# One hybrid transformer step: four mixers and their projections move from the framework's scheduler into the kernel's own list schedule

## The chip, the cores and the metric

The kernel runs on one core of a Trainium2 chip. The core has five engines, each with its own in-order stream: TensorE (PE, matmuls, with PEld for the loading of weights), VectorE (DVE), ScalarE (ACT), GpSimd (POOL) and SyncE (SP), which here issues nearly all transfers. The metric is the device time of one execution in microseconds (us).

## The reference

The reference computes one layer of a diffusion backbone on 128 context tokens and 512 latent tokens (640 rows of 1024 values):

```
h    = rmsnorm(x) * (1 + scale1) + shift1          # shift, scale, gate: silu(c) @ ada_w
proj = h @ w_in                                     # 1024 x 3360, split among four mixers
A: HGRN2 gated linear recurrence, both directions   (q, i, f_fwd, f_bwd, g)
B: GLA gated linear attention, both directions      (q, k, v, g, a_fwd, a_bwd)
C: RG-LRU recurrence after a 4-tap convolution      (x, gate)
D: short convolution, b * conv(c * v)
x = x + gate1 * (concat(A, B, C, D) @ w_out)
x = x + gate2 * (relu(rmsnorm(x)-modulated @ w1)^2 @ w2)
y = rmsnorm(x)
```

It returns y for all rows and the final states of A, B and C. Every matmul works on fp32 data; the large ones split each operand into a rounded part and a remainder and add three products (hi x hi, hi x lo, lo x hi).

## The kernel before, in words

**Three stages.** In the first one, up to about 58 us, the rows are normalised, transposed and modulated into `hhi` and `hlo` (the two parts of h, with channels on the partitions), and two of the thirteen projections (`a0`, `q`) are computed in a PE order that is written out by hand (`START`). The second stage, from 58 to 325 us, holds the other projections and the four mixers. The third holds the output projection, the second norm and the MLP.

**The second stage.** Each projection chunk is 256 columns of `w_in`. `need` loads it (SP, tile `raw...`), `prep` makes `hi...` and `lo...` of it on ACT or DVE, and `proj_cm` multiplies it with `hhi` and `hlo`: 48 matmuls of 320 columns for 128 outputs, into one of two PSUM buffers of the tag `mm` (tiles `pj...`; `v...` for values). A `use_...` function then reads that buffer out: `use_db`, for example, is three DVE multiplications from PSUM (L848 to L850). The mixers A (two jobs) and B (one job of two head pairs) run a recurrence as a tree of eight levels, 1 to 128: at each level copies build `K` and `Qb` from the array `G` (on ACT or DVE, by the table `ON_DVE`), PE computes scores `sA` or `sB` with small matmuls, DVE merges them under a mask (`copy_predicated` into `W`) and multiplies `G` by the decays (L944, L945). After level 128 come the state updates (`kt`, `ds`, `St`), the readout `o` and a norm over heads (`hn`). C has small block matmuls (`rg`), activations and scans. `ada` units compute the modulation vectors with matmuls (`ap`).

**Two kinds of matmul on PE.** A projection uses all 128 columns of the array. The scores, the `ap` matmuls, `pjba` and parts of `ds` and `o` write 32 or 64 partitions only, and two or four of these run side by side on different columns.

**What sets the order.** The list `PLAN` says in which order the units are written: a projection unit such as `cx0`, or one step of a job (`A0`, `A1`, `RG`, `B`). In the kernel before, the units of `PLAN` are handed straight to the framework, whose scheduler orders the instructions of each engine. The third stage is different: its operations are recorded in a `Plan`, a list scheduler inside the kernel. `cost` gives each operation a duration by formulas, `record` keeps it with its operands, `add` finds which earlier operations touch the same elements, and `emit` computes for each operation the latest time at which it must begin, walks through time, and at each moment gives the engine that is free first the ready operation with the least such time. `Late` tiles stand for tiles that are allocated only when they are emitted. `Slots` are the buffers of a tag, in the order in which their users were recorded. What `emit` puts out is kept in that order (`manual_schedule`). In the third stage the order on PE is fixed by the program (`plan.chain`).

**The weights of the output projection.** `wo_v` and `wo_x` load `w_out` through two buffers `w2raw` and four buffers `wq`, on the same SP queue as the projections' weights.

Of the kernel before, what the change touches and what calls it, by code (L numbers as in the profile page):

```python
# [13 lines left out]
D = 1024  # L14
# [131 lines left out]
class Plan:  # L146

    def __init__(self, nc, like):  # L150
        self.nc, self.like, self.ops, self.seen, self.masks = nc, like, [], {}, {}
        self.chain, self.last_pe, self.hint, self.tiles_of = False, None, None, {}
# [80 lines left out]
    def record(self, eng, fn, op, a, k):  # L233
# [12 lines left out]
        def go():  # L246
            r = lambda x: x.real() if isinstance(x, Late) else x
            return fn(*[r(x) for x in a], **{w: r(v) for w, v in k.items()})  # L248

        return self.add(eng, dur, go, ins, outs, mb, sets)  # L250

    def add(self, eng, dur, fn, ins=(), outs=(), mb=0.0, sets=None, after=()):
# [16 lines left out]
        for k in keys:  # L269
            if isinstance(k, LateTile):  # L270
                if not k.users:
                    k.slots.queue.append(k)
                    if k.pool.opened is not None:
                        order.add(k.pool.opened)
                k.users.append(i)
                k.pool.users.append(i)
# [16 lines left out]
    def emit(self):  # L293
# [115 lines left out]
def hybrid_step_kernel(ctx: ExitStack, tc: tile.TileContext, A: dict, O: dict):  # L409
# [42 lines left out]
    def lnexp(after):  # L452
        with tc.issue_after(after.ins):
            ld = act.preload_act_table_set("natural_log_exp_and_others")
        with tc.issue_after(ld.ins):
            yield

# [251 lines left out]
    me_, ml_ = ExitStack(), ExitStack()  # L709
    me = me_.enter_context(tc.tile_pool(name="mixe", bufs=1, reuse_waits="tile"))  # L710
    mp = ml_.enter_context(tc.tile_pool(name="mixl", bufs=1, side="right", reuse_waits="tile"))

# [5 lines left out]

    def sub(t, g, off, ap):
        v = t[:, g, off:off + 1]  # L720
        return bass.AP(tensor=v.tensor, offset=v.offset, ap=[list(v.ap[0])] + ap)
# [488 lines left out]
    for u in PLAN:  # L1210
# [10 lines left out]
        if u == "q1":  # L1221
            psS_stack.close()
            psB = stB.enter_context(tc.tile_pool(name="psB", bufs=2, space=PS, reuse_waits="tile"))
    grow1 = gate_rows("gt1", nc.sync)
    for j in jobs.values():
        assert next(j, None) is None
    me_.close()
    lp = ctx.enter_context(tc.tile_pool(name="mlp", bufs=1, reuse_waits="tile"))
    oT["hi"] = [lp.tile([128, 2, T], F32R, name=f"ohi{i}", tag=f"ohi{i}") for i in range(4)]
    oT["lo"] = [lp.tile([128, T], F32R, name=f"olo{i}", tag=f"olo{i}") for i in range(8)]  # L1230
    for j in range(2):
        put_o(4 + j, [(slice(0, 128), hs[j][:, 0:128]), (slice(128, T), hs[j][:, 134:646])])
# [4 lines left out]
    for j in range(2):  # L1237
        put_o(6 + j, [(ALL, dd["o", j])])
    ml_.close()
    hw_.close()  # L1240
    plan = Plan(nc, par[:, 0:1].tensor)
    rp = LatePool(plan, ctx.enter_context(tc.tile_pool(name="mlpr", bufs=1, side="right", reuse_waits="tile")))
    ls = LatePool(plan, ctx.enter_context(tc.tile_pool(name="mlps", bufs=1, reuse_waits="tile")))
    stB.close()
    psA_.close()
    psN = LatePool(plan, ctx.enter_context(tc.tile_pool(name="psN", bufs=1, space=PS, reuse_waits="tile")), psum=True)
    lp = LatePool(plan, lp)
    VH, VL = ([lp.tile([128, D], F32R, name=f"{nm}{i}", tag=f"{nm}{i}") for i in range(4)] for nm in ("vh", "vl"))
    BIG = [lp.tile([128, D], F32, name=f"big{i}", tag=f"big{i}") for i in range(2)]
    WRAW2 = [lp.tile([128, D], F32, name=f"w2raw{i}", tag=f"w2raw{i}") for i in range(2)]  # L1250
    act, dve, pe, pool, sync = (Now(e) for e in (act, dve, pe, pool, nc.sync))

# [32 lines left out]
    def wo_x(i, k0):  # L1285
        for k in range(2):
            s = [k0 + 2 * k, k0 + 2 * k + 1]
            wo[2 * i + k] = [(XH[j], XL[j]) for j in s]
            for n, j in enumerate(s):
                raw = WQ[2 * k + n]  # L1290
                sync.dma_start(raw, A["wout"][i][:, D * k + 512 * n:D * k + 512 * n + 512])
                split(XH[j], XL[j], raw)

    def wo_v(i, k0):
        for k in range(2):
            j = k0 + k
            sync.dma_start(WRAW2[k], A["wout"][i][:, D * k:D * k + D])
            split(VH[j], VL[j], WRAW2[k])
# [5 lines left out]
    wo_x(3, 4)  # L1304
    act, dve, pe, pool = plan.engines()
    nc = Queues(plan, nc)
    last_used = [2, 0, 3, 1]
# [455 lines left out]
```

## Time and profile before

| what | value |
|---|---|
| median of 3 runs | 824.52 us (822.47 to 827.32) |
| profiled execution: its own time | 819.71 us |
| profiled execution: span | 817.9 us |
| PE busy | 778.8 us, 95% |
| DVE busy | 575.2 us, 70% |
| ACT busy | 420.3 us, 51% |
| granted clock of PE, mean | 0.997 |

The times of the table are of whole executions; the trace is of one of them, and its span runs from its first instruction to its last, 1.8 us less than its own time. A busy share is the union of an engine's instructions. The rows of the trace name an engine, a line (L249 or L248 is the line of the recording layer, through which many operations go), an operation, and the tile written and the tiles read, without buffer numbers.

### The profile page before, as it was taken

The numbers are of one execution on the slowest core, as the hardware profiler recorded it, in microseconds if no ns is written. First come the engines' busy times: TensorE is split into PE (matmuls) and PEld (weight loads), VectorE is DVE, ScalarE is ACT, GpSimd is POOL, SyncE is SP. The second block draws the span as 40 slices with busy tenths as digits, with TensorE's granted clock in tenths as the row PEclk, the third lists the DMA queues.
The fourth block names the chain that finished last, engine by engine and source line by source line (L and its number), as shares of the span: only waits on it lengthen the run. The fifth ranks groups of instructions, "written<-read, shape, count | busy, mean of one in ns | idle before, by whom it ended". The sixth has DMA issues, their size and how long they took to land.

```text
span 817.9 us, 13749 instructions
## 1 busy us (share of the span) xinstructions
PE 778.8 (95%) x5536; PEld 682.7 (83%) x5536; DVE 575.2 (70%) x1061; ACT 420.3 (51%) x708; POOL 23.4 (3%) x48
## 2 busy tenths in 40 slices
PE   4999999999999989999899999899999999999995
PEld 3798988768777889888888989789899898998984
DVE  4779988857786376368997888647466475675757
ACT  7533549688486332156784706417246172371533
POOL 0040000101010000000000000000000000000001
PEclk9999999999999999999999999999999999999998
DMA  9723323333321522543653636513132041330313
GB/s 352 304 83 137 105 95 142 116 110 100 125 84 56 104 103 65 194 155 127 204 165 102 195 97 204 119 40 117 50 131 75 20 136 52 101 106 2 128 52 128
DMA packets 33696, 97.79 MB, mean 120 GB/s; under 512 B 8672, under 2 KB 9696, under 8 KB 29024
## 3 DMA queue, kind: packets, MB, share of 16 engines
q1 hardware_dynamic: 32544, 95.72, 35.5%
q10 hardware_dynamic: 576, 1.00, 0.4%
q8 instruction: 43, 0.70, 0.3%
q0 software_dynamic: 512, 0.20, 0.1%
q14 instruction: 21, 0.17, 0.1%
HBM read 91.44 MB, written 5.46 MB: 118 GB/s over the span
## 4 chain that ended last, share of the span: by engine, by line
PE 63%; DVE 15%; ACT 10%; DMA 8%; issue 3%; SPq 0%; DVEq 0%; ACTq 0%
PE ps L248 45%; DMA wq<-in_w_dram 4%; ACT QbB L462 2%; DVE xl L248 2%; PE pjcx L492 2%; PE pjdb L492 2%; PE pja L666 2%; DMA w2raw<-in_wout_dram 1%; PE ap L536 1%; DVE wq L248 1%; DMA w2raw<-in_w_dram 1%; PE pjbqk L492 1%; DVE big L248 1%; PE rg L1132 1%; DMA rawdb<-in_win_dram 1%
## 5 line engine op out<-in xcount | busy, mean ns | idle before, releaser
L248 PE MATMUL ps<-vh,olo 128*128 128x512 f32 x680 | 186.4, 390 | 1.0 <-DVE olo L248 0.7
L248 PEld LDWEIGHTS ps<-vh,olo 128*128 128x128 f32 x680 | 126.9, 188 | 28.8 <-DVE olo L248 1.9
L248 PE MATMUL ps<-vl,olo 128*128 128x512 f32 x320 | 99.3, 390 | 0.0
L248 ACT ACTIVATE vh<-w2raw 128x1024 fp32r<-128x1024 f32 x32 | 33.8, 1057 | 118.6 <-PE ps L248 114.2
L248 ACT ACTIVATE xh<-wq 128x512 fp32r<-128x512 f32 x96 | 59.4, 628 | 61.1 <-PE ps L248 43.9
L248 PE MATMUL ps<-yh,xh 128*128 128x320 f32 x256 | 79.5, 311 | 1.2 <-DVE rb L248 1.2
L248 PE MATMUL ps<-yl,xh 128*128 128x320 f32 x256 | 79.0, 309 | 0.0
L248 PE MATMUL ps<-yh,xl 128*128 128x320 f32 x256 | 79.0, 308 | 0.0
L248 DVE TENSOR_TENSOR h<-ps,h 128x512 f32<-128x512 f32 x60 | 38.6, 686 | 52.9 <-PE ps L248 52.6
L248 PEld LDWEIGHTS ps<-vl,olo 128*128 128x128 f32 x320 | 60.1, 188 | 12.7
L248 DVE TENSOR_TENSOR xl<-wq,xh 128x512 fp32r<-128x512 f32 x96 | 64.8, 687 | 8.1 <-ACT xh L248 7.9
L248 PE MATMUL ps<-ohi,xh 128*128 128x320 f32 x256 | 57.1, 310 | 0.5 <-ACT xh L248 0.4
L248 ACT ACTIVATE rb<-rb 128x640 f32<-128x640 f32 x64 | 46.8, 734 | 7.6 <-DVE rb L248 6.8
L248 PEld LDWEIGHTS ps<-yh,xh 128*128 128x128 f32 x256 | 48.1, 188 | 2.0 <-DVE rb L248 1.5
L248 PEld LDWEIGHTS ps<-yl,xh 128*128 128x128 f32 x256 | 48.1, 188 | 0.3
L248 PEld LDWEIGHTS ps<-yh,xl 128*128 128x128 f32 x256 | 48.1, 188 | 0.0
L248 DVE TENSOR_TENSOR vl<-w2raw,vh 128x1024 fp32r<-128x1024 f32 x32 | 39.0, 1220 | 8.1 <-ACT vh L248 7.4
L248 PEld LDWEIGHTS ps<-ohi,xh 128*128 128x128 f32 x256 | 42.8, 188 | 1.1 <-ACT xh L248 0.6
L248 PE MATMUL ps<-ohi,xl 128*128 128x320 f32 x128 | 39.8, 311 | 0.5 <-DVE xl L248 0.4
L248 DVE TENSOR_TENSOR olo<-rb,olo 128x640 fp32r<-128x640 f32 x32 | 26.3, 821 | 18.6 <-ACT olo L248 18.6
L248 PE MATMUL ps<-t,xh 128*128 128x320 f32 x128 | 28.7, 311 | 0.7 <-DVE rb L248 0.7
L248 ACT ACTIVATE rb<-ps 128x320 f32<-128x320 f32 x64 | 27.1, 424 | 4.1 <-PE ps L248 4.1
(426 smaller groups left out, 1677.7 us busy)
## 6 DMA issues: line engine op xcount, KB each, us to landing
ar<-in_ada_w_dram SPq DMA_DIRECT2D x20, 1024.0 KB, 4.9
wq<-in_w_dram SPq DMA_DIRECT2D x72, 256.0 KB, 3.7
w2raw<-in_w_dram SPq DMA_DIRECT2D x32, 512.0 KB, 4.4
big<-in_ada_g_dram SPq DMA_DIRECT2D x8, 512.0 KB, 3.5
x<-in_x_dram SPq DMA_DIRECT2D x5, 512.0 KB, 6.8
big<-in_x_dram SPq DMA_DIRECT2D x5, 512.0 KB, 4.2
x1d<-big SPq DMA_DIRECT2D x5, 512.0 KB, 2.6
xa<-x1d SPq DMA_DIRECT2D x5, 512.0 KB, 4.5
```

What stands on the lines that cost most here:

```text
L248: return fn(*[r(x) for x in a], **{w: r(v) for w, v in k.items()})
L462: act.activation(out, src, AF.Copy)
L492: pe.matmul(ps[:, n, :320], wt[:, k, c0:c0 + 128], h[:, k, s], start=(k == 0 and wt is hi and h is hhi), stop=stop)
L536: pe.matmul(ps[32 * g:32 * g + 32, :256], scx[:, 4 * j + g, 2 - 2 * vi:34 - 2 * vi], r3[:, 4 * j + g, :], start=(vi == 0 and j == 0), stop ...
L666: pe.matmul(d, w[:, k, 128 * j:128 * j + 128], (hlo if hi_ else hhi)[:, k, c], start=begin, stop=end, skip_group_check=(ch == "q" and i == 1))
L1132: pe.matmul(ps, wrg[:, dl, j, g, :], xc[:, hN * n:hN * n + hN], start=True, stop=True)
```

## The change

The `Plan` is made before the mixers, and everything from the second stage on is recorded in it: the projections with their loads and splits, the mixers, the `ada` units, the output projection and the MLP. The two pools of the mixers, the weight pool and the PSUM pools become `LatePool`s. Pools that are closed and opened between the stages become events in the plan: `open_lp` after the last operation that uses the pool `me`, `open_rest` and `open_psum` after the last ones of the others.

- The projections that the first stage leaves unread get release times (`ready`: "pja0" at 7.5, "pjq" at 18.4 us on the plan's own clock), and the engines get the times at which they come free (`free`).
- The first operation that uses a tile must now stand before its others, and when several tiles share one buffer, a tile is due no later than the next one's first use.
- The table loads for logarithms on ACT are no longer placed by hand; `lnexp` sets a hint.
- `ON_DVE` is the same, so each copy stays on its engine. The PE order is free in the second stage and fixed in the third, as it was. No operation is added or left out, but for ACT's table loads, of which 27 stand in the program where 29 stood.

```
-    def __init__(self, nc, like):
+    def __init__(self, nc, like, ready=(), free=None):
+        self.ready, self.free, self.first = dict(ready), dict(free or {}), {}
...
+        for x in ins:
+            if not isinstance(x, Late):
+                for name, t in self.ready.items():
+                    if x.tensor.name.startswith(name):
+                        self.first[len(self.ops)] = t
...
+                elif k.users[0] != i:
+                    order.add(k.users[0])
...
+        before = {}
+        for x in slots:
+            for p, q in zip(x.queue, x.queue[1:]):
+                before.setdefault(q.users[0], []).append(p.users[0])
         for i in range(n - 1, -1, -1):
             eng, dur, _, deps, order, mb, _ = ops[i]
+            for d in before.get(i, ()):
+                if d < i:
+                    latest[d] = min(latest[d], latest[i])
...
-        at, free, ready, end_of = [0.0] * n, {}, {}, [0.0] * n
+        at, free, ready, end_of = [self.first.get(i, 0.0) for i in range(n)], dict(self.free), {}, [0.0] * n
...
+    plan = Plan(nc, par[:, 0:1].tensor, ready={"pja0": 7.5, "pjq": 18.4}, free={"PE": 18.2, "ACT": 7.5, "DVE": 8.4})
+    me = LatePool(plan, me_.enter_context(tc.tile_pool(name="mixe", bufs=1, reuse_waits="tile")))
+    mp = LatePool(plan, ml_.enter_context(tc.tile_pool(name="mixl", bufs=1, side="right", reuse_waits="tile")))
+    real_nc, const0 = nc, const
+    act, dve, pe, pool = plan.engines()
+    nc = Queues(plan, nc)
+    const, wpool, psA = LatePool(plan, const0), LatePool(plan, wpool, bufs=2), LatePool(plan, psA, psum=True, bufs=2)
...
+    def open_psum():
+        stB.close()
+        psA_.close()
+        psN.real = ctx.enter_context(tc.tile_pool(name="psN", bufs=1, space=PS, reuse_waits="tile"))
+
+    rp.opened = ls.opened = plan.event(open_rest, [lp.opened] + wpool.users + mp.users + on_rows)
+    psN.psum = True
+    psN.opened = plan.event(open_psum, psA.users + psB.users + on_first)
```

How the order moves is shown at three places.

**The readout of mixer B's second head pair, on PE.** `oB` is the readout; its `64x128` matmuls write one half of the partitions each, and two of them make a pair. `pjdc`, `pjdb` and `pjdv` are projections of mixer D. Before:

```order
L1053 MATMUL oB_3041<-TB_2118,vbv 64x128 x2
L1047 MATMUL oB_3041<-GB,StB_2771 128x128
L1049 MATMUL oB_3041<-GB,StB_2771 128x128
L1053 MATMUL oB_3041<-TB_2118,vbv 64x128 x2
L492 MATMUL pjdc_3061<-hlo,hidc 128x320
```

Now the readout stands near the end of the stage, among two projections that alternate:

```order
L249 MATMUL pjdb_3381<-hhi,hidb 128x320
L249 MATMUL oB_3299<-TB_2724,vbv 64x128
L249 MATMUL pjdb_3381<-hhi,hidb 128x320
L249 MATMUL oB_3299<-TB_2724,vbv 64x128
L249 MATMUL pjdv_3342<-hlo,hidv 128x320
L249 MATMUL oB_3299<-GB,StB_2315 128x128
L249 MATMUL pjdb_3381<-hlo,hidb 128x320
L249 MATMUL pjdv_3342<-hlo,hidv 128x320
```

A pair that stood together is parted by a projection's matmul, and two projections are computed in turns where before one ended ahead of the other.

**The SP queue at the end of the stage.** `rawdv` and `rawdb` are the last two weight chunks of the projections, `w2raw` and `wq` the weights of the output projection, `rowgt` a row of gates, `big` rows of x. Before:

```order
L472 DMA rawdv<-in_win_dram 128x2048
L561 DMA rowgt_3476<-gt_76 128x8x1 x2
L130 DMA w2raw_3529<-in_wout_dram 128x1024
L130 DMA w2raw_3535<-in_wout_dram 128x1024
L130 DMA w2raw_3529<-in_wout_dram 128x1024
L130 DMA w2raw_3535<-in_wout_dram 128x1024
L472 DMA rawdb<-in_win_dram 128x2048
```

Now:

```order
L249 DMA rawdv<-in_win_dram 128x2048
L249 DMA rawdb<-in_win_dram 128x2048
L249 DMA rowgt_611<-gt_76 128x8x1 x2
L249 DMA w2raw_3419<-in_wout_dram 128x1024
L249 DMA w2raw_3423<-in_wout_dram 128x1024
L249 DMA big_3425<-in_x_dram 128x1024
```

`rawdb` no longer stands behind four loads of `w_out`.

**The join of the second and the third stage, on PE.** `hnb` is the head norm of mixer B, `pjdb` the last projection, and `ps` the output projection. Before, `hnb` stands 78 projection matmuls ahead of this piece's last row:

```order
L492 MATMUL pjdb_3423<-hhi,hidb 128x320 x2
L492 MATMUL pjdb_3423<-hlo,hidb 128x320 x2
L492 MATMUL pjdb_3423<-hhi,lodb 128x320 x2
L248 MATMUL ps_0_3605<-vh_3531,ohi_3485 128x512
L248 MATMUL ps_1_3613<-vh_3531,ohi_3485 128x512
```

Now:

```order
L249 MATMUL pjdv_3342<-hhi,lodv 128x320
L249 MATMUL pjdb_3381<-hhi,lodb 128x320
L249 MATMUL pjdb_3381<-hhi,hidb 128x320 x2
L249 MATMUL pjdb_3381<-hlo,hidb 128x320 x2
L249 MATMUL pjdb_3381<-hhi,lodb 128x320 x2
L249 MATMUL pjdb_3381<-hhi,hidb 128x320 x2
L249 MATMUL pjdb_3381<-hlo,hidb 128x320 x2
L249 MATMUL hnb_3519<-o2b_3451,con 128x320
L249 MATMUL hnb_3524<-o2b_3451,con 128x320
L249 MATMUL pjdb_3381<-hhi,lodb 128x320 x2
L249 MATMUL pjdb_3381<-hhi,hidb 128x320 x2
L249 MATMUL pjdb_3381<-hlo,hidb 128x320 x2
```

After two more matmuls of `pjdb` the row `ps_0` follows. The projection `pjdv`, which ended 48 matmuls before `ps`, ends 19 matmuls and the two of `hnb` before it. From that row to the end PE's order is the same in both kernels.

## Rows read from the trace of the kernel before

**Rows 1.** Busy time by stage: PE, PEld, DVE, ACT, POOL, granted clock, DMA share, GB/s.
```profile
0.00:58.20 58.20, 45.42 (x368) 38.62 (x369) 36.75 (x87) 32.38 (x56) 10.00 (x25) 1.00 0.64 254
58.20:325.00 266.80, 254.81 (x2587) 218.30 (x2586) 201.09 (x388) 154.98 (x248) 10.95 (x22) 1.00 0.31 101
60.00:160.00 100.00, 97.92 (x1248) 86.35 (x1248) 92.19 (x189) 58.15 (x96) 4.08 (x6) 1.00 0.36 125
325.00:420.00 95.00, 91.65 (x489) 79.53 (x489) 70.80 (x128) 52.28 (x103) 0.00 (x0) 1.00 0.51 174
420.00:817.90 397.90, 386.95 (x2098) 346.21 (x2097) 266.59 (x460) 180.62 (x302) 2.41 (x1) 0.99 0.32 99
```

**Rows 2.** Waits of PE, 58.2 to 325 us: total, times, longest (us).
```profile
PE sB L962 <- ACT QbB L462: 3.1, 7, 0.7
PE pjdb L492 <- DVE lodb L483: 1.4, 1, 1.4
...
PE sB L989 <- issue: 0.9, 2, 0.7
PE pjdb L492 <- DVE hidb L460: 0.9, 1, 0.9
PE sA L962 <- DVE QbA L460: 0.8, 2, 0.5
...
PE sB L962 <- DVE QbB L460: 0.5, 2, 0.3
PE sA L989 <- ACT QbA L462: 0.5, 1, 0.5
PE pjdv L492 <- DVE sgb L813: 0.5, 1, 0.5
```

**Rows 3.** SP's issues, 40 to 340 us: start, length of the group, queue, transfer.
```profile
274.02 14.41 SPq L130 DMA_DIRECT2D w2raw<-in_wout_dram  x4
290.96 0.33 SPq L472 DMA_DIRECT2D rawdb<-in_win_dram  x1
```

**Rows 4.** Timeline of PE, first and last of a `pjdb` stretch: start, length, instruction.
```profile
317.93 0.46 PE L492 MATMUL pjdb<-hhi,hidb 128*128 128x320 f32 x2
...
324.68 0.46 PE L492 MATMUL pjdb<-hhi,lodb 128*128 128x320 f32 x2
324.97 0.63 PE L248 MATMUL ps<-vh,ohi 128*128 128x512 f32 x2
```

**Rows 5.** Timeline of PE, one score block among projections.
```profile
64.96 0.46 PE L492 MATMUL pja<-hhi,loa 128*128 128x320 f32 x2
65.35 0.77 PE L962 MATMUL sA<-QbA,KA 128*32 128x64 f32 x40
66.05 0.56 PE L492 MATMUL pja<-hhi,hia 128*128 128x320 f32 x2
66.44 0.45 PE L492 MATMUL pja<-hlo,hia 128*128 128x320 f32 x2
```

**Rows 6.** Timeline of PE, two score blocks that follow each other.
```profile
92.05 0.28 PE L863 MATMUL vi<-loi,hhi 128*128 128x256 f32 x1
92.17 0.28 PE L864 MATMUL vi<-hii,hlo 128*128 128x256 f32 x1
92.38 1.32 PE L962 MATMUL sA<-QbA,KA 128*32 128x64 f32 x80
93.63 0.56 PE L492 MATMUL pjcx<-hhi,hicx 128*128 128x320 f32 x2
94.03 0.46 PE L492 MATMUL pjcx<-hlo,hicx 128*128 128x320 f32 x2
```

**Rows 7.** Timeline of PE, a level of mixer B and what it waits for.
```profile
205.74 0.85 PE L962 MATMUL sB<-QbB,KB 128*32 128x128 f32 x20 [0.61 <-ACT QbB L462]
```

**Rows 8.** Timeline of DVE, the readout of the last two projections of mixer D.
```profile
318.13 0.29 DVE L832 TENSOR_TENSOR du<-dc,pjdv 128x128 f32<-128x128 f32 x1 [0.26 <-PE pjdv L492]
...
319.79 1.84 DVE L840 SCALAR_TENSOR_TENSOR dy<-du,par,dy 128x656 f32<-128x656 f32 x2
325.17 0.29 DVE L848 TENSOR_TENSOR od<-dy,pjdb 128x128 f32<-128x128 f32 x1 [3.55 <-PE pjdb L492]
...
325.64 0.48 DVE L850 TENSOR_TENSOR od<-dy,pjdb 128x320 f32<-128x320 f32 x1
```

**Rows 9.** Timeline of PE and of DVE: mixer B's head norm.
```profile
309.63 1.24 PE L1071 MATMUL hnb<-o2b,con 128*128 128x320 f32 x4
312.89 0.82 DVE L1077 TENSOR_TENSOR orB<-orB,o2b 128x640 f32<-128x640 f32 x1
```

More of the change, by code (lines that the diff above doesn't have):

```diff
@@ L452, in lnexp @@
     def lnexp(after):
[L453 to L456, printed above, removed]
+        plan.hint = "natural_log_exp_and_others"
+        yield
+        plan.hint = None
     def cp(name, out, src):
@@ L709, in hybrid_step_kernel @@
     me_, ml_ = ExitStack(), ExitStack()
-    me = me_.enter_context(tc.tile_pool(name="mixe", bufs=1, reuse_waits="tile"))
-    mp = ml_.enter_context(tc.tile_pool(name="mixl", bufs=1, side="right", reuse_waits="tile"))
+    plan = Plan(nc, par[:, 0:1].tensor, ready={"pja0": 7.5, "pjq": 18.4}, free={"PE": 18.2, "ACT": 7.5, "DVE": 8.4})
[5 more added lines that the diff above has]
+    const, wpool, psA = LatePool(plan, const0), LatePool(plan, wpool, bufs=2), LatePool(plan, psA, psum=True, bufs=2)
     def tmp(nm):
@@ L719, in sub @@
     def sub(t, g, off, ap):
+        if isinstance(t, Late):
+            return t.view(lambda x: sub(x, g, off, ap))
         v = t[:, g, off:off + 1]
@@ L1221, in hybrid_step_kernel, with open_psB, open_lp @@
         if u == "q1":
-            psS_stack.close()
-            psB = stB.enter_context(tc.tile_pool(name="psB", bufs=2, space=PS, reuse_waits="tile"))
+            def open_psB():
+                psS_stack.close()
+                psB.real = stB.enter_context(tc.tile_pool(name="psB", bufs=2, space=PS, reuse_waits="tile"))
+            psB = LatePool(plan, psum=True, bufs=2)
+            psB.opened = plan.event(open_psB, range(len(plan.ops)))
     grow1 = gate_rows("gt1", nc.sync)
+    on_rows = on_first = list(range(len(plan.ops)))
     for j in jobs.values():
         assert next(j, None) is None
-    me_.close()
-    lp = ctx.enter_context(tc.tile_pool(name="mlp", bufs=1, reuse_waits="tile"))
+    lp, rp, ls, psN = (LatePool(plan) for _ in range(4))
+    def open_lp():
+        me_.close()
+        lp.real = ctx.enter_context(tc.tile_pool(name="mlp", bufs=1, reuse_waits="tile"))
+    lp.opened = plan.event(open_lp, me.users)
     oT["hi"] = [lp.tile([128, 2, T], F32R, name=f"ohi{i}", tag=f"ohi{i}") for i in range(4)]
     oT["lo"] = [lp.tile([128, T], F32R, name=f"olo{i}", tag=f"olo{i}") for i in range(8)]
+    VH, VL = ([lp.tile([128, D], F32R, name=f"{nm}{i}", tag=f"{nm}{i}") for i in range(4)] for nm in ("vh", "vl"))
+    BIG = [lp.tile([128, D], F32, name=f"big{i}", tag=f"big{i}") for i in range(2)]
+    WRAW2 = [lp.tile([128, D], F32, name=f"w2raw{i}", tag=f"w2raw{i}") for i in range(2)]
     for j in range(2):
@@ L1238, in hybrid_step_kernel, with open_rest @@
         put_o(6 + j, [(ALL, dd["o", j])])
[L1239 to L1251, printed above, removed]
+    def open_rest():
+        ml_.close()
+        hw_.close()
+        rp.real = ctx.enter_context(tc.tile_pool(name="mlpr", bufs=1, side="right", reuse_waits="tile"))
+        ls.real = ctx.enter_context(tc.tile_pool(name="mlps", bufs=1, reuse_waits="tile"))
+    def open_psum():
[5 more added lines that the diff above has]
+    psN.opened = plan.event(open_psum, psA.users + psB.users + on_first)
     HT = T // 2
@@ L1290, in wo_x @@
                 raw = WQ[2 * k + n]
-                sync.dma_start(raw, A["wout"][i][:, D * k + 512 * n:D * k + 512 * n + 512])
+                nc.sync.dma_start(raw, A["wout"][i][:, D * k + 512 * n:D * k + 512 * n + 512])
                 split(XH[j], XL[j], raw)
@@ L1296, in wo_v @@
             j = k0 + k
-            sync.dma_start(WRAW2[k], A["wout"][i][:, D * k:D * k + D])
+            nc.sync.dma_start(WRAW2[k], A["wout"][i][:, D * k:D * k + D])
             split(VH[j], VL[j], WRAW2[k])
@@ L1304, in hybrid_step_kernel @@
     wo_x(3, 4)
-    act, dve, pe, pool = plan.engines()
-    nc = Queues(plan, nc)
     last_used = [2, 0, 3, 1]
```

## The prediction

> **What bounds the kernel now.** I read the busy time by stage first [rows 1]. The changed code ends at 325 us: from the first matmul of the output projection on, PE's order is the same, and the reader is to see that these stages (95.00 and 397.90 us) are PE's already, with 91.65 and 386.95 us busy. The first stage, 58.20 us, keeps its hand-written order. So the change is decided in the second stage: 266.80 us long, PE busy for 254.81. All that a better order can win there by filling PE's holes is 266.80 - 254.81 = 12.0 us. DVE is busy for 201.09 and ACT for 154.98 us of it; but between 60 and 160 us DVE is busy for 92.19 of 100 us beside PE's 97.92, so there the kernel has a second engine without slack.
>
> Next the waits of PE in that stage [rows 2]. Two kinds are to be seen. The waits of a score block for the copies `QbA` and `QbB` that come before it sum to 3.1 + 0.9 + 0.8 + 0.5 + 0.5 = 5.8 us (the 0.9 is put down to "issue", but it is the first matmul of the same blocks). The waits of `pjdb` for its split weights sum to 1.4 + 0.9 = 2.3 us. The SP queue tells why [rows 3]: four loads of `w_out` take 14.41 us from 274.02 on, and `rawdb` is issued only at 290.96.
>
> Last the timeline of PE, for prices. A projection matmul of 320 columns in a plain stretch costs (324.97 - 317.93) / 48 = 0.147 us [rows 4]. A score block among projections costs more than its own work at both of its ends: from 64.96 to 66.44 us stand four projection matmuls and one block of 40 small ones, so the block costs 1.48 - 4 x 0.147 = 0.89 us, and 0.39 - 0.29 = 0.10 of that lies before its first matmul [rows 5]. Two blocks side by side, 80 small matmuls, cost 1.74 - 0.29 = 1.45 us from 92.29 on (92.38 less the part before the first matmul) [rows 6], where two by themselves cost 2 x 0.89 = 1.78. One more excursion from wide matmuls to packed ones and back is thus worth 1.78 - 1.45 = 0.33 us.
>
> **The change part by part.** The sum is made against the profiled execution, 819.71 us (span 817.9). The median of the runs is 824.52, a factor 1.0059 above it, and the sum is carried over by that factor.
>
> (1) *The weights of D.* `rawdb` is now issued ahead of the loads of `w_out`, right behind `rawdv`, so both waits of `pjdb` go: -2.3 us [rows 2, 3]. What comes late in its stead are the loads of `w_out`, which begin when PE still has both projections of the end before it, more than the 14.41 us that the four take. Bounds: -2.3 and 0.
>
> (2) *The waits for the copies of Q.* Each step of the mixers is now placed by its own operations, and projection matmuls are put between the levels where the framework left PE waiting, as in the 0.61 us at 205.74 [rows 7]. The operations of the mixers come at about the same distance in PE work as before, so the copies themselves are not earlier; what hides the wait is projection work, and there is enough of it while projections last. The levels of B that fall behind the last free chunk keep theirs. I take two thirds of 5.8: -3.9 us. Bounds: -5.8 and 0.
>
> (3) *The two alternating kinds of matmul.* In the order before, PE leaves the 128-column matmuls for packed ones 59 times between the second A projection and `ps`; now it does so 79 times, since a list scheduler that picks the most urgent ready operation cuts blocks apart: pairs of `oB` and `oA`, runs of `sB`, and `pjba` are now parted by single projection matmuls, as the first piece of order shows. No row shows a block cut in this way, so the price is bounded by what the ends of a whole block cost: 0.10 us for the way in alone, 0.33 for one whole excursion [rows 5, 6]. 20 excursions give +2.0 to +6.6 us. I take 0.33, since that row compares just the two cases (two blocks together, two apart): +6.6.
>
> The Trainium skill, "TensorEngine Tiling (Array Packing)", section Key Properties, says that a change of the tiling mode, unlike a change of tile within one mode, drains TensorE. By that rule, each of the 20 excursions drains it twice; the 0.10 us in front of a block and the 0.33 us for a whole excursion [rows 5, 6] agree with it in kind. Without such a price the term would be 0 and the sum at the end -1.3 us; with it the sum is as given there.
>
> (4) *Projections in turns.* Before, one projection ends 7 us (48 x 0.147) ahead of the next, and the reading out of its PSUM buffer lies beside the next one's matmuls. There are only two buffers. Now five pairs of projections alternate on PE, so both buffers are filled at about the same time, and the third projection must wait for a reader. What one such wait costs is bounded by the one of that kind that the trace has, `pjdv` for a gate's activation, 0.5 us [rows 2], and by an eviction that begins only then, `od` from 325.17 to 326.12 us, 0.95 us [rows 8]. I count four such joints, the fifth being the end of the stage, at 0.7 each: +2.8 us. Bounds: 0 where packed work fills the joint, and +3.8.
>
> (5) *The end of the stage.* The first `ps` now takes the PSUM banks that `pjdb` leaves, so it waits for `od`, DVE's reading of `pjdb`; before, it waited for nothing of the kind. From the end of `pjdv` PE has 19 projection matmuls and two of `hnb` left: 19 x 0.147 + 1.1 = 3.9 us (the two `hnb` at 309.63 us are a group of four rows and took 1.24 from begin to end, some 1.1 from begin to begin [rows 9]). DVE has, from the same moment, `du` and `dy`, 318.13 to 321.63 us, 3.5 us, then 0.8 for B's normalisation `orB` [rows 9], then 0.95 for `od` [rows 8]: 5.3 us, of which `od` must also lie behind the last matmul of `pjdb`. PE stands still for 5.3 - 3.9 = 1.4, with the step between engines about +1.5 us. Bounds: 0.95 (only `od` is late) and 3.5. Behind `ps` the whole rest of PE waits, so nothing hides it.
>
> (6) *Other new holes.* More splits of weights stand close to their first use; I give them +0.6 us, with bounds 0 and +3, the 1.4 us of one late `lodb` [rows 2] twice.
>
> At nothing I cost two table loads fewer on ACT, which is busy for 154.98 of 266.80 us, and the recording layer itself, which adds no instruction. The granted clock is 1.00 in the stage [rows 1] and the change leaves PE as busy as it was, so no other level of the clock comes in.
>
> Sum: -2.3 - 3.9 + 6.6 + 2.8 + 1.5 + 0.6 = +5.3 us. 819.7 + 5.3 = 825.0 for an execution like the profiled one, times 1.0059: 829.8 us.
>
> **The rivals.**
>
> *Faster: the holes are filled and cutting blocks costs little.* If PE takes a cut block at the price of the way in alone, 0.10 us, and packed work fills the joints, then all of the 5.8 us goes: -5.8 - 2.3 + 2.0 + 1.5 = -4.6, that is 815.1, by the factor 819.9 us. For it: PE's queue of ready work is long up to 300 us, and the 0.10 is a row. Against it: the comparison of one double block with two single ones gives three times as much. It decides from a price below about 0.15 us for an excursion together with no wait at the joints.
>
> *Slower: DVE's own order.* In its queue, mixer A's first job now has the multiplication of `G` at level 2 behind the elementwise work of the second job, and that waits for a projection of a pair which ends together. An in-order engine holds everything behind such an instruction, up to one projection's 7 us, while it has 8 us of slack in 100 between 60 and 160 us [rows 1]. Two such places, 14 us, lost on DVE and then on PE's score blocks, which wait for it: 833.7, by the factor 838.6 us. Against it: projections can run in the meantime as long as a PSUM buffer is free. It decides if PE's idle time between 60 and 160 us passes 5 us (2.1 before).
>
> *Nothing: PE was the bound and stays so.* The milestones of the mixers lie within a few us of PE work of where they stood (B's levels 3 to 5 us later), so gains and losses could both be one or two us: 824.5 us. For it: 95% of the stage is PE's already. Against it: the 20 more excursions are in the order, not an estimate.
>
> **How the numbers follow.** Forecast 0.48 (its own terms give +1 to +10 us), the faster rival 0.25, DVE's order 0.15, nothing 0.12. A measurement of this kernel can tell about 0.5%, 4.1 us, from no change. Of the forecast's 0.48, about a third lies under +4.1 us: 0.17 there and 0.31 above. So slower has 0.31 + 0.15 = 0.46, the same 0.17 + 0.12 = 0.29, faster 0.25. The range goes from 817, a little below the faster rival, to 842, a little above DVE's order; the likeliest case by itself spans 825.5 to 834.6.
>
> **What would show it.** In the profile after: (1) no wait of `pjdb` for `hidb` or `lodb`; (2) the waits of `sB` and `sA` for `Qb...` below 2 us in all instead of 5.8; (3) PE's busy time in the stage grown by the excursions, since time at their ends shows as longer matmuls or short gaps: the time of the stage less its waits above 259 us; (4) waits of first matmuls of projections for readers such as `sg...`, `vi` or `od`, about 0.7 each; (5) the first `ps` waits 1 to 2 us for DVE's `od`; (6) a stage of about 272 us, with the two others as long as they were. The forecast is wrong in its sign if the stage is shorter than 266 us: then look at (3), the price of a cut block, first; it is wrong in its size if DVE shows idle time behind a wait for PE between 60 and 160 us.

## The result and the profile after

The changed kernel is slower: median 835.44 us against 823.5 (four runs of each; the 824.52 above is of the first three), ratio 1.0148 (95% interval 1.0103 to 1.0193). In a second series (run 5 below) it took 836.95 against 821.53, ratio 1.0185 (1.014 to 1.0231). Its profiled execution took 839.11 us, the longest of its four runs, with a span of 837.3; the three others lie at 835.4 to 835.5.

The busy time by stage of the kernel after, with the columns of [rows 1]:

```profile
0.00:58.70 58.70, 46.13 (x368) 39.48 (x369) 35.39 (x84) 32.19 (x55) 9.94 (x25) 1.00 0.70 269
58.70:341.50 282.80, 264.87 (x2587) 222.96 (x2585) 195.34 (x387) 151.31 (x246) 11.59 (x22) 0.99 0.28 94
60.00:160.00 100.00, 93.91 (x1205) 81.41 (x1203) 83.75 (x163) 55.73 (x86) 3.21 (x5) 1.00 0.29 104
```

The second stage is 282.8 us long where it was 266.8 [rows 1]: 16.0 of the 19.4 us between the two spans. The first stage grew by 0.5 and the third by 2.9. In the second stage PE's idle time grew from 12.0 to 17.9 us, and its busy time, for the same matmuls, from 254.8 to 264.9. So most of the loss, 10.1 us, is in time in which PE counts as busy, and no wait shows it.

PE's waits in that stage after the change (total, times, longest in us):

```profile
PE pjbg L249 <- ACT gelu L249: 4.5, 1, 4.5
PE rg L249 <- DVE StA L249: 2.0, 2, 1.0
PE ps L249 <- DVE od L249: 1.6, 1, 1.6
PE oB L249 <- DVE StB L249: 1.4, 1, 1.4
PE oA L249 <- ACT gi L249: 1.4, 1, 1.4
PE ap L249 <- DMA ar<-in_ada_w_dram: 1.4, 1, 1.4
PE dsB L249 <- DVE StB L249: 1.2, 1, 1.2
PE pjdv L249 <- DVE sgb L249: 1.1, 1, 1.1
PE sA L249 <- ACT QbA L249: 0.7, 1, 0.7
...
PE vi L249 <- DVE vi L249: 0.6, 1, 0.6
...
PE pjcg L249 <- ACT vbv L249: 0.5, 1, 0.5
```

The waits of [rows 2] for the copies of Q are gone but for 0.7 us, and so are both of `pjdb`. New is one long stop, 4.5 us at `pjbg`. The timeline of PE around it:

```profile
247.22 0.82 PE L249 MATMUL pjcg<-hhi,locg 128*128 128x320 f32 x4
252.54 0.90 PE L249 MATMUL pjbg<-hhi,hibg 128*128 128x320 f32 x2 [4.49 <-ACT gelu L249]
253.24 0.73 PE L249 MATMUL pjbg<-hlo,hibg 128*128 128x320 f32 x2
253.77 0.73 PE L249 MATMUL pjbg<-hhi,lobg 128*128 128x320 f32 x2
```

Both `pjcg` buffers end together, and `pjbg` needs one of them. A row here is a pair of matmuls. Behind the stop two pairs begin 0.53 us apart (253.24 to 253.77) instead of 0.29 as in [rows 4]. The reason is seen in windows of 1 us, where the column behind POOL's busy time is the granted clock:

```profile
250.00:251.00 1.00, 0.00 (x0) 0.00 (x0) 0.95 (x3) 0.98 (x2) 0.00 (x0) 1.00 0.98 410
251.00:252.00 1.00, 0.00 (x0) 0.00 (x0) 0.95 (x4) 0.99 (x2) 0.00 (x0) 0.65 1.01 426
253.00:254.00 1.00, 1.00 (x5) 1.00 (x5) 1.00 (x2) 0.99 (x3) 0.00 (x0) 0.50 0.00 0
258.00:259.00 1.00, 1.00 (x13) 0.83 (x10) 1.00 (x1) 0.55 (x1) 0.00 (x0) 0.94 0.00 0
259.00:260.00 1.00, 1.00 (x9) 0.99 (x8) 1.00 (x1) 0.98 (x3) 0.00 (x0) 1.00 0.00 0
```

Within the stop the granted clock fell from 1.00 to 0.50 (2.4 to 1.2 GHz) and it was back at 1.00 from 259 on. PE's busy time there times the missing share of the clock, summed over the windows, is 2.8 us: what the low clock cost. ACT shows why `gelu` was late:

```profile
248.05 0.74 ACT L249 ACTIVATE o2a<-orA 128x640 f32<-128x640 f32 x1
248.81 0.90 ACT L249 ACTIVATE TB<-sB 32x64 f32<-32x64 f32 x4
249.73 0.74 ACT L249 ACTIVATE o2a<-orA 128x640 f32<-128x640 f32 x1
250.49 1.28 ACT L419 ACT_TABLE_LOAD   x1
251.78 0.70 ACT L249 ACTIVATE gelu<-pjcg 128x640 f32<-128x640 f32 x1
```

ACT was at work without a break, 3.7 us from 248.05 on, with operations that the schedule had put ahead of the one that PE needed.

Taking the 2.8 us off, PE's busy time in the stage is 264.7 - 2.8 = 261.9 us (between the end of `pjq` and the first `ps`) against 254.6. I call this the full-clock work in what follows. The remaining 7.3 us I put down to the cuts between packed and wide matmuls; the runs below test this. An excursion is one way from wide matmuls to packed ones and back. The timeline of PE at the second readout of `oB` shows some of them:

```profile
321.88 0.46 PE L249 MATMUL pjdv<-hhi,hidv 128*128 128x320 f32 x2
322.17 0.36 PE L249 MATMUL pjdb<-hhi,hidb 128*128 128x320 f32 x1
322.46 0.43 PE L249 MATMUL oB<-TB,vbv 128*64 128x128 f32 x2
322.82 0.42 PE L249 MATMUL pjdb<-hhi,hidb 128*128 128x320 f32 x1
323.17 0.43 PE L249 MATMUL oB<-TB,vbv 128*64 128x128 f32 x2
```

One projection matmul takes from 322.82 to 323.17, 0.35 us, where 0.147 is its price in a plain stretch: the other 0.20 us belong to the change of kind, and none of these rows has a wait. What the engine does in this time no row tells.

The end of the stage came as forecast: PE waits 1.55 us for `od`, behind `orB`. The timeline of PE, then that of DVE:

```profile
339.47 0.46 PE L249 MATMUL pjdb<-hhi,lodb 128*128 128x320 f32 x2
341.48 0.70 PE L249 MATMUL ps<-vh,ohi 128*128 128x512 f32 x2 [1.55 <-DVE od L249]
```

```profile
338.65 0.82 DVE L249 TENSOR_TENSOR orB<-orB,o2b 128x640 f32<-128x640 f32 x1
339.38 0.90 DVE L249 SCALAR_TENSOR_TENSOR dy<-du,par,dy 128x656 f32<-128x656 f32 x1
340.39 0.95 DVE L249 TENSOR_TENSOR od<-dy,pjdb 128x128 f32<-128x128 f32 x3
```

### The profile page after: what moved, and what is told of

Read it like the earlier page. It is cut to its first block, busy times and chain, and to the rows that moved or that the text cites. A ratio compares the mean times of both kernels' runs of the same rounds, so it can differ in the third digit from the quotient of the medians.

```text
span 837.3 us, 13751 instructions
## 1 busy us (share of the span) xinstructions
PE 789.3 (94%) x5536; PEld 688.3 (82%) x5536; DVE 572.9 (68%) x1061; ACT 417.9 (50%) x706; POOL 23.9 (3%) x48
## 4 chain that ended last, share of the span: by engine, by line
PE 52%; DVE 8%; DMA 4%; issue 1%; ACT 1%; SPq 0%; DVEq 0%; ACTq 0%
PE ps L249 46%; DMA wq<-in_w_dram 3%; DVE xl L249 2%; PE pjdv L249 1%; DMA w2raw<-in_w_dram 1%; PE pjdb L249 1%; DVE wq L249 1%; PE pjdc L249 1%; PE pjbg L249 1%; PE oB L249 1%; DVE vl L249 1%; DVE olo L249 1%; DVE big L249 1%; DVE rb L249 1%; DMA big<-in_ada_g_dram 0%
## 5 line engine op out<-in xcount | busy, mean ns | idle before, releaser
L249 ACT ACTIVATE xh<-wq 128x512 fp32r<-128x512 f32 x104 | 64.6, 628 | 73.5 <-PE ps L249 43.5
L249 ACT ACTIVATE vh<-w2raw 128x1024 fp32r<-128x1024 f32 x36 | 38.0, 1057 | 118.7 <-PE ps L249 113.7
L249 DVE TENSOR_TENSOR xl<-wq,xh 128x512 fp32r<-128x512 f32 x104 | 70.1, 687 | 14.2 <-ACT xh L249 13.9
L249 DVE TENSOR_TENSOR vl<-w2raw,vh 128x1024 fp32r<-128x1024 f32 x36 | 43.9, 1221 | 7.8 <-ACT vh L249 7.2
```

## The experiments

All kernels compute the whole step. The table sums up their second stage, from the end of `pjq` to the first `ps`, each from its profiled execution: excursions counted in the order; idle time of PE; loss by a low clock (worked out as above); full-clock work, which is the busy time less that loss. The ratio is to the kernel before. Runs 1 to 4 ran on one chip, 5 to 8 on a second, 9 to 11 on a third, each time beside the kernel before, whose median was 819.46, 821.53 and 821.76 us; so kernels of different chips are compared by their ratios.

| kernel | excursions | stage | idle | low clock | full-clock work | median | ratio (95%) |
|---|---|---|---|---|---|---|---|
| before | 59 | 266.6 | 12.0 | 0 | 254.6 | | |
| changed | 79 | 282.6 | 17.9 | 2.8 | 261.9 | 835.44 | 1.0148 (1.010, 1.019) |
| 1 in turn | 83 | 289.6 | 24.4 | 2.3 | 262.9 | 844.34 | 1.0299 (1.028, 1.032) |
| 2 readers | 77 | 276.8 | 14.5 | 0 | 262.3 | 834.00 | 1.0175 (1.015, 1.020) |
| 3 cut | 136 | 311.5 | 16.9 | 4.3 | 290.2 | 865.39 | 1.0565 (1.054, 1.059) |
| 4 in turn, kept | 65 | 286.2 | 23.7 | 6.9 | 255.5 | 842.29 | 1.0279 (1.026, 1.030) |
| 5 changed, again | 79 | 281.7 | 17.9 | 2.3 | 261.6 | 836.95 | 1.0185 (1.014, 1.023) |
| 6 as 4, loads behind | 65 | 282.9 | 21.8 | 5.4 | 255.7 | 836.33 | 1.0183 (1.013, 1.024) |
| 7 margin | 80 | 276.1 | 13.4 | 1.7 | 261.0 | 836.13 | 1.0176 (1.012, 1.023) |
| 8 as 6, margin | 58 | 278.3 | 21.8 | 3.5 | 253.0 | 832.05 | 1.0143 (1.009, 1.020) |
| 9 early, kept | 60 | 267.0 | 12.1 | 1.7 | 253.2 | 827.03 | 1.0077 (1.005, 1.011) |
| 10 early | 70 | 267.4 | 9.8 | 0 | 257.6 | 825.48 | 1.0039 (1.001, 1.007) |
| 11 no release | 63 | 286.5 | 24.7 | 4.7 | 257.1 | 841.59 | 1.0250 (1.019, 1.031) |
| 12 before, again | 59 | 266.8 | 12.1 | 0 | 254.6 | 820.73 (one run) | |

**1. Projections in turn.**

```
+            n0 = len(plan.ops)
             (proj_ba if c == "ba" else proj_cm)(ps, wts[c], 128 * j, 256, hhi, hlo)
+            in_turn(n0)      # first matmul of a unit after the last one of the unit before
```

> The changed kernel, with one more rule: on PE the projections are computed one after another (the first matmul of a projection's unit comes after the last one of the unit before). Theory A (the loss is in projections that alternate: both PSUM buffers end together, PE stands still at pjbg for 4.5 us, and the granted clock falls behind that stop; and 0.33 us for each of the 74 excursions to packed matmuls instead of 79): no stop over 2 us at pjbg, clock 1.00 throughout, so 835.4 - 4.5 - 3.3 - 1.1 - 5 x 0.33 = about 825 us. Theory B (the list schedule places work of ACT and DVE late, whatever the order of the projections): other waits of the same size take their place, 833 to 837 us.

Measured 844.34 us, the wrong way. The stop at `pjbg` is gone, but a longer one stands at `pjdb`, on PE:

```profile
309.27 0.46 PE L249 MATMUL pjdv<-hhi,lodv 128*128 128x320 f32 x2
320.29 0.90 PE L249 MATMUL pjdb<-hhi,hidb 128*128 128x320 f32 x2 [10.56 <-DVE hidb L249]
```

Theory A fails as far as it calls the alternation itself the loss; theory B's kind of wait took its place, larger than it said. (The rule also covers the value projections, and the order has 83 excursions, not the 74 of the expectation; its full-clock work, 262.9 us, is right for 83.) On SP `rawdb` now stands behind other loads:

```profile
292.36 0.36 SPq L249 DMA_DIRECT2D rawdv<-in_win_dram  x1
296.24 1.02 SPq L249 DMA_DIRECT2D rowgt<-gt  x2
297.37 1.05 SPq L249 DMA_DIRECT2D w2raw<-in_wout_dram  x2
299.73 7.30 SPq L249 DMA_DIRECT2D big<-in_x_dram  x2
307.14 0.59 SPq L249 DMA_DIRECT2D rawdb<-in_win_dram  x1
```

**2. Readers first.**

```
+        if eng in ("ACT", "DVE") and any(isinstance(x, Late) and x.tile.args[3] == "mm" for x in ins):
+            self.reads_mm.add(i)
...
+            for x in xs:
+                if x in self.reads_mm:
+                    latest[x] -= 8.0
+                    self.reads_mm.discard(x)
```

> The changed kernel, with the operations of ACT and DVE that read a projection's PSUM buffer due 8 us earlier than the list scheduler has them; the projections still alternate, 77 excursions instead of 79. Theory A (one late reader, gelu, makes the stop at pjbg and the fall of the clock): the stop shrinks below 2 us, the clock stays at 1.00, 835.4 - 3 - 3.3 - 0.7 = about 828 us. Rival (the clock falls for a reason other than that stop): the stop is gone and the clock still falls, about 831 to 832. Theory B (work on ACT is only exchanged, another operand is late): 834 to 837.

The stop at `pjbg` shrank from 4.5 to 1.13 us, the clock stayed at 1.00 in the whole stage, and the stage is 5.8 us shorter than the changed kernel's: this fall of the clock goes with this stop. On PE:

```profile
248.24 0.56 PE L250 MATMUL pjbg<-hhi,hibg 128*128 128x320 f32 x2 [1.13 <-ACT gelu L250]
248.64 0.45 PE L250 MATMUL pjbg<-hlo,hibg 128*128 128x320 f32 x2
```

In the whole time this does not show: the ratio, 1.0175, is within the intervals of the changed kernel's two series, whose third stage was 495.9 and 495.1 us against 497.1 here, with 1.7 us lost to a fall of the clock at 545 us. So theory A is right in its mechanism and wrong in its time. The 834.00 us lie in theory B's range, but its exchange is not seen: without the stop at `pjbg` PE is idle for 13.4 us in both kernels (17.9 - 4.5 and 14.5 - 1.1).

**3. More cuts.**

`packed` holds the matmuls that write fewer than 128 partitions.

```
+            elif eng == "PE":
+                i = min(xs, key=lambda x: (latest[x] + (-2.0 if (x in self.packed) != kept else 0.0), x))
+                kept = i in self.packed
```

> The changed kernel, with the list scheduler made to prefer (by 2 us of due time) a change between packed and 128-column matmuls on PE: 136 excursions instead of 79, 77 of them single packed matmuls. Theory A (0.33 us for each excursion): 835.4 + 57 x 0.33 = about 854 us, and PE's busy time in the second stage grows by 19 us. Rival (0.10 us, the way in alone): about 841 us. Rival (a cut costs nothing, PE's longer stage has other reasons): 835, waits aside.

865.39 us, above theory A's 854. The full-clock work grew by 290.2 - 261.9 = 28.3 us for 57 more excursions, 0.50 each; PE's busy time in the stage, by the window below, grew by 29.7.

```profile
58.60:370.10 311.50, 294.59 (x2585) 231.63 (x2583) 197.54 (x389) 152.61 (x247) 11.93 (x22) 0.98 0.24 85
```

77 of the 136 excursions are single packed matmuls, whose partner no longer runs beside them; in the changed kernel 14 of 79 are. That they cost more for this reason is likely and was not measured apart. Both cheap rivals fall.

**4. In turn and kept together.** The first run's rule, and the third run's line with +4.0 in place of -2.0.

> The changed kernel, with projections one after another as in the first of these runs, and with packed and 128-column matmuls each kept together (a change of kind counts 4 us in due time): 59 excursions, as many as in the kernel before. Theory A: the losses of the change are alternation and cuts, so both undone give 835.4 - 8.9 - 20 x 0.33 = about 820 us. Rival (cuts cost 0.10): about 824 to 825. Theory B (late work on ACT and DVE): 830 or more.

842.29 us: theory A is wrong in the sum and right in one term, and theory B's time, 830 or more, is met. The order has 65 excursions (not 59), and the full-clock work is back at 255.5. The time went to 23.7 us of waits (8.9 of them `pjdb` for `hidb`) and to the low clock, 6.9 us: 3.5 behind that stop and 3.4 behind a stop of 1.5 us at 187.5.

**5. The changed kernel again.**

> The changed kernel itself once more, beside the three that follow, so that they are compared on one chip. Ratio to the kernel before as it was, 1.0148 (1.010 to 1.019), with the stop at pjbg of about 4.5 us, the low clock behind it, and a second stage near 283 us.

1.0185, the stop 4.5 us, the stage 281.7: the same picture.

**6. Loads of w_out behind rawdb.**

```
             nc.sync.dma_start(WRAW2[k], A["wout"][i][:, D * k:D * k + D])
+            plan.ops[-1][4].add(dbload[0])      # in SP's order behind the load rawdb
```

> The fourth run's kernel (projections in turn, packed and wide matmuls kept together; its order has 65 excursions) with one rule more: on SP the loads of the output projection's weights are issued behind the load rawdb. Theory (the stop of 8.9 us at pjdb in that run is a load queued behind others, and the low clock after 310 us is that stop's): both go, 842.3 less 8.9, 1.6 and some 3.5 for the clock, about 828 us where the kernel before takes 819.5. Rival (rawdb waits for its buffer, not for the queue): the stop stays, 840 or more.

836.33 us; the stop is still 7.6 us, so the loads of `w_out` were a small part of it. The ratio fell from 1.0279 to 1.0183; in the profiles the second stage is 3.3 us shorter and the third 5.3. The stop stayed, as the rival said, but its time (840 or more) was not reached, and its reason is only half of what the eighth run, which has the same rule, shows. On SP:

```profile
284.75 0.36 SPq L251 DMA_DIRECT2D rawdv<-in_win_dram  x1
288.26 1.02 SPq L251 DMA_DIRECT2D rowgt<-gt  x2
289.38 1.11 SPq L251 DMA_DIRECT2D big<-in_x_dram  x2
293.97 0.33 SPq L251 DMA_DIRECT2D rawdb<-in_win_dram  x1
```

and on DVE:

```profile
291.65 2.29 DVE L251 TENSOR_TENSOR lodv<-rawdv,hidv 128x2048 fp32r<-128x2048 f32 x1
306.56 1.23 DVE L251 CAST hidb<-rawdb 128x2048 fp32r<-128x2048 f32 x1 [9.06 <-DMA rawdb<-in_win_dram]
```

There is one buffer of raw weights: `rawdb` can be loaded when `lodv` has read `rawdv` (293.9). That is the rival's half. `rawdv` itself, due just before its use, was issued only after the last `ap` matmul had read the `ar` in that buffer, at 284.3.

The other half is the transfer: 12.6 us (293.97 to 306.56), where `rawdv` took 4.9. By an estimate from these two, at 4.9 us `hidb` would have been ready at about 300.1, before PE was through with `pjdv` at 300.7, and the stop of 7.1 us would not be there. What differs is what was issued ahead of the load. `rowgt` is two loads of 4 KB that took 11.7 us to land, and `big`, next behind it, took 13.6. In the runs 1, 4, 6 and 8 `rawdb` was issued 5.7 to 10.9 us behind `rowgt` and took 11.5 to 13.0 us; in the changed kernel and the runs 2, 3, 5, 7, 9, 10 and 11 it was issued ahead of `rowgt`, or 15.6 us behind it, and took 4.7 to 5.4. The loads of `w_out` right behind it did not slow it: runs 3 and 11 have them there too. Whether `rowgt` does it alone or only with `big` was not tried.

**7. Margin for PE.**

`early` holds PE's operations of the second stage.

```
-                    d = end + hop[eng]
+                    d = end + hop[eng] + (1.0 if j in self.early and not mb else 0.0)
```

> The changed kernel with one number changed: in the second stage the list scheduler reckons each result of ACT or DVE as reaching PE 1 us later than before. Projections still alternate, 80 excursions. Theory C (half of the new waits are small matmuls of the mixers that stand at the head of PE's queue for operands a little later than reckoned: rg, oA, oB, dsB, some 6 us, and the stop at pjbg): the waits of the stage fall from 17.9 to about 11 us and the clock stays at 1.00, 6 to 10 us faster than the changed kernel, a ratio to it of about 0.99. Rival (waits only move, for PE has no other work ready): within 3 us of the changed kernel. PE's full-clock work stays at 262 us, since the excursions do.

In the profile, which is of the fastest of the four runs, the waits fell to 13.4 us and the stage to 276.1. The runs spread from 831.58 to 840.34: 836.13 against 836.95 for the changed kernel beside it, the rival's "within 3 us". Theory C's 6 to 10 us are not seen, though the spread is wide. The full-clock work stayed, as it should, at 261.0. The clock did not stay at 1.00; it fell once, for 1.7 us' worth, with no long stop ahead of it (windows of 1 us as above):

```profile
186.39:187.39 1.00, 0.48 (x7) 0.32 (x7) 0.97 (x3) 0.89 (x3) 0.19 (x1) 1.00 0.00 0
187.39:188.39 1.00, 1.00 (x15) 0.63 (x15) 1.00 (x4) 0.99 (x2) 0.00 (x0) 0.56 0.00 0
188.39:189.39 1.00, 1.00 (x10) 0.82 (x5) 1.00 (x3) 0.99 (x1) 0.00 (x0) 0.50 0.00 0
```

The last stop before it was 1.6 us (`sB` for `QbB`, to 186.9). Behind the longest stop of this run, 2.9 us (`sB` for `TB`, to 257.3), the clock stayed at 1.00. So a stop shorter than that of `pjbg` may or may not bring the low clock.

**8. All of these.** The sixth and the seventh run's rules.

> The sixth and the seventh run's rules together: in turn, kept together, rawdb ahead, and 1 us of margin for PE; 58 excursions, one fewer than in the kernel before. If the price of an excursion (some 0.37 us by the runs so far) and the waits are the whole loss, PE's full-clock work returns to 255 us, the waits are about 12 us, and the kernel takes what the one before takes, ratio 0.995 to 1.005. Rival (other losses in the list schedule's order): ratio above 1.01.

832.05 us, 1.0143: above the range of the first theory, and the rival's. The full-clock work came out under the kernel before (253.0 with 58 excursions); the waits did not (21.8, of them 7.1 for `hidb`), and the clock fell behind that stop (3.5 us).

**9. Holders of scarce buffers early, and kept together.** The second run's lines with 15.0 us, for every operation that loads or reads the raw weight buffer or reads a projection's PSUM; with the margin, the order of loads and +2.0 for a change of kind. Projections alternate.

```
+        if any(isinstance(x, Late) and (x.tile.args[3] == "wraw" or x.tile.args[3] == "mm" and eng in ("ACT", "DVE"))
+               for x in list(ins) + (list(outs) if eng == "SP" else [])):
+            self.reads_mm.add(i)
```

> Projections alternate as in the changed kernel. Added to it: packed and wide matmuls kept together (2 us of due time), 1 us of margin for PE's operands, the loads of w_out behind rawdb, and everything that holds the one buffer of raw weights (loads, splits, ada matmuls) or reads a projection's PSUM is due 15 us earlier. 60 excursions. Theory D (the two losses are the number of excursions and holders of scarce buffers that are due as late as the plan allows): full-clock work near 255 us, no stop above 3 us, clock 1.00, the second stage 264 to 269 us, ratio to the kernel before 0.995 to 1.005. Rival (the list schedule loses for other reasons as well): ratio above 1.010.

**10. The same without keeping together.**

> The kernel before this one in the list without the rule that keeps packed and wide matmuls together: 70 excursions instead of 60, the rest the same. By a price of 0.37 us an excursion PE's full-clock work is 10 x 0.37 = 3.7 us more, about 258.5 us, and the kernel 3 to 4 us longer. If an excursion costs the way in alone (0.10): 1 us longer, not to be told apart.

827.03 (1.0077) and 825.48 us (1.0039), where the kernel before took 821.76: about three quarters of the changed kernel's loss (1.0148 and 1.0185 in its two series) are undone in the tenth, about half in the ninth. The stages of the ninth and the tenth run, in windows:

```profile
58.50:325.60 267.10, 254.97 (x2586) 219.94 (x2585) 189.68 (x379) 148.45 (x243) 11.51 (x22) 0.99 0.29 95
```

```profile
59.00:326.50 267.50, 257.66 (x2586) 219.93 (x2585) 193.41 (x383) 150.96 (x245) 11.85 (x22) 1.00 0.31 99
```

Both are as long as in the kernel before [rows 1]. Theory D holds for the second stage, though the clock fell once in the ninth (1.7 us). In the whole time the ninth, with a third stage of 500.1 us (498.2 in the tenth, 493.0 before), is above theory D's range and below the rival's 1.010; the tenth would lie in that range. The ten excursions cost 257.6 - 253.2 = 4.4 us of work, near the 3.7 expected. The kernel did not get longer by that: the tenth waits 2.3 us less and lost nothing to the clock, so it is the shorter. The fall in the ninth stands behind a stop of 2.0 us (`pjbqk` for `vi`); the same stop of 2.1 us in the tenth brought none. Neither beats the kernel before.

**11. No release times.**

```
-    plan = Plan(nc, par[:, 0:1].tensor, ready={"pja0": 7.5, "pjq": 18.4}, free={"PE": 18.2, "ACT": 7.5, "DVE": 8.4})
+    plan = Plan(nc, par[:, 0:1].tensor)
```

> The changed kernel without release times and without the times at which the engines come free (the plan begins as if all were at hand at zero); 63 excursions instead of 79 come out. By the price of 0.37 us the full-clock work is 262 - 16 x 0.37 = about 256 us; if the waits stay near 18 us and the stop at pjbg with its clock stays, the second stage is about 276 us and the kernel 6 us faster than the changed one. Rival (the release times are what the order needs, without them operands are late): waits above 22 us, no faster than the changed kernel.

841.59: the rival held. The full-clock work is 257.1 with 63 excursions, but the waits are 24.7 us, the first of them 6.7 of `pja` for `hia` at the stage's start. So the two sets of times together are a part of the change that helps, as far as the profiles go; the interval of the ratio overlaps with that of run 5.

**12. The kernel before again.**

> The kernel before once more, for a second trace of it. If its third stage is 493 us again (waits of ps for olo and rb of some 2 us together, no fall of the clock), the 2 to 7 us that the other kernels' third stages took more belong to their order; if it is 496 or more, they are how much that stage differs from run to run, and the whole difference of the changed kernel lies in the second stage, 266.6 us here again.

Second stage 266.8, third 493.6. The changed kernel's third stage, 495.9 and 495.1 in two executions, is some 2 us longer, but not for one reason. In the first, `ps` waits 6.5 us for `olo` and `rb`, against 2.9 and 4.3 in the two traces of the kernel before. In the second these waits are 4.2, and 1.6 us are a fall of the clock at 546 us behind a stop of 1.8. So it is not shown that the 2 us belong to the order. In the third stages of the other kernels 1.5 to 3.1 us are such falls, but for the ninth's, which has none.

## Why the prediction was right or wrong

The direction and the range (817 to 842) hold; the size was off: +5.3 us forecast for an execution like the profiled one, and 11.9 between the medians (15.4 in the second series), 19.4 between the profiled spans. That the range holds is in part luck. The forecast's own terms ended at 834.6 us, below the 835.44 measured; the range goes on to 842 for the rival of DVE's order, which is not what cost the time. The second stage's 16.0 us by the terms:

| term | forecast | measured | from |
|---|---|---|---|
| (1) weights of D | -2.3 | -2.3 | no wait of `pjdb` |
| (2) waits for Q | -3.9 | -5.1 | 5.8 less 0.7 |
| (3) excursions | +6.6 | +7.3 | full-clock work 254.6 to 261.9 |
| (4) joints | +2.8 | +6.2 | 4.5 + (1.1 - 0.5) + 0.6 + 0.5 |
| (5) end of the stage | +1.5 | +1.6 | `ps` for `od` |
| (6) new holes | +0.6 | +5.5 | the other waits, 8.6 less 3.1 |
| clock | 0 | +2.8 | 251 to 259 us |

Three terms came out above their own bounds, (3) by 0.7, (4) by 2.4 and (6) by 2.5 us, and the clock had been given none.

**Right: the excursions.** The price read from one pair of rows, 0.33 us [rows 5, 6], became 0.37 in the changed kernel (7.3 / 20), and a straight line through the eleven orders of 58 to 83 excursions has a slope of 0.39, none off it by more than 1.7 us. Cuts cost time although no matmul was added. The rule of the Trainium skill ("TensorEngine Tiling (Array Packing)", Key Properties) that a change of tiling mode drains TensorE agrees with this in kind; no row here tells a drain from another loss at the cut. The price grew to 0.50 where single packed matmuls were cut out. The faster rival, with 0.10 us, fell by this.

**Wrong: the joints and what comes behind them.** The step "I count four such joints ... at 0.7 each" took the wait from a reader that is free when the projection ends. At `pjbg` the reader was not free: ACT had 3.7 us of other work ahead of `gelu`, a table load among it. The three other joints cost 0.5 to 0.6 more each, near the 0.7 assumed. The sentence "no other level of the clock comes in" is the second error: one stop of 4.5 us brought 0.50 for some 7 us, and what I had looked at, PE's mean busy share, does not tell that. In the second run both went together. But falls are not tied to long stops alone: in the runs 4, 6, 7 and 9 the clock also fell behind stops of 1.5 to 2.0 us.

**Wrong: new holes.** Waits of `rg`, `oA`, `oB`, `dsB`, `ap` and one of `pjbqk` came to 8.6 us; in the trace of before, those of `ap`, `rg` and `dsB` are 3.1. I had given them 0.6, thinking of splits of weights only. Six stops of 1.0 to 1.4 us stand at such small matmuls (`rg` twice, `oA`, `oB`, `dsB` and `ap`), each at the head of PE's queue when its operand was late.

**The rivals.** DVE's order cost far less than its rival said, though its mechanism is in the trace. Its mark, more than 5 us of idle PE between 60 and 160 us, was reached (6.1). DVE did stand still behind PE's results, 5.9 us at `FA` (to 75.5 us, through ACT, for the pair `pja` that ends together) and 3.8 us at `red` (to 133.1, for `ap`), and was busy for 83.75 us there instead of 92.19. But PE had projections to go on with: the score block behind `FA` waited 0.7 us, and PE's waits for DVE there are 3.8 us in all (`rg` 2.0 and three of 0.6), not 14. That nothing would change is out by the interval.

**What the cause is, as far as shown.** The second stage comes back to its old length when excursions are fewer and, at the same time, whatever holds the raw buffer or a projection's PSUM is due earlier (runs 9 and 10). Parts of it did not do it: fewer excursions without the buffers (4, 6, 8) left the waits, the longest of them behind the slow load that run 6 tells of, which in runs 9 and 10 was issued ahead of `rowgt`; readers of PSUM 8 us earlier (2) and a margin alone (7) left the excursions. Which part of the early rule matters most, buffers of weights or of PSUM, was not separated, and the rule was not run without the margin and the order of loads. The third stage's 2 us stay open.

## What to carry to other kernels

Count in the new order how often TensorE goes from wide to packed matmuls and back, and price that from two rows of the old trace: it showed as busy time, in no list of waits, and was the largest term. In a list schedule, ask of every buffer with one or two copies what its reader has ahead of it on its own engine; the due time of an operation must count what waits for its buffer, and not only who reads its result. Look at the granted clock behind each stop of TensorE: in these runs every stop of 4.4 us or more in the second stage cost its own length and then 2 to 4 us for the low clock behind it. And look at what stands ahead of an urgent load in its queue: in the runs 1, 4, 6 and 8 a load of 1 MB issued behind two loads of 4 KB and two of `big` took some 7 us more.

## What was not expected of the hardware

A stop of 4.5 us on PE brought some 7 us at the lower level of the granted clock, 0.50, in two executions, and stops of 10.6, 8.9, 7.6, 7.1, 6.7, 4.6 and 4.4 us in other runs brought such a fall likewise. Below that, length alone does not tell: stops of 1.5, 1.6 and 2.0 us (runs 6, 7 and 9) were followed by some 3 us at 0.50, with PE busy throughout, and stops of 1.8, 2.9 and 2.1 us (runs 6, 7 and 10) were not.

`rowgt`, two loads of 4 KB, took 10.6 us to land in run 3 with no other load under way. The 1 MB load `rawdb` took 11.5 to 13.0 us where it was issued while `rowgt` was under way, and 4.7 to 5.4 in the other orders of the list schedule.
